# A two-layer encoder trunk: another way out of PSUM for three tiles at the end of the delta-rule layer, and the fourth weight block of the MLP split earlier

## The chip, the cores and the metric

The kernel runs on one core of a Trainium2 chip. The metric is the device time of one execution in microseconds (us). An execution here takes 1306 us; a change under 0.2% of that, 2.6 us, cannot be told from none.

## What is computed

The reference is an encoder trunk of four residual layers on an input of 512 tokens by 1024 features, in float32. Each layer is followed by a LayerNorm over a scaled residual:

```
for i in range(DEPTH):                       # DEPTH = 2
    m = _mixer_gdn(x, ...) if i % 2 == 0 else _mixer_gla(x, ...)
    x = _layernorm(DEEPNORM_ALPHA * x + m, ln1_g[i], ln1_b[i])
    x = _layernorm(DEEPNORM_ALPHA * x + _sq_relu_mlp(x, mlp_w1[i], mlp_w2[i]), ln2_g[i], ln2_b[i])

def _layernorm(x, g, b):
    mu = jnp.mean(x, axis=-1, keepdims=True)
    xc = x - mu
    var = jnp.mean(xc * xc, axis=-1, keepdims=True)
    return xc * lax.rsqrt(var + LN_EPS) * g + b

def _mixer_gdn(h, w_in, conv_w, a_log, dt_bias, norm_g, w_out):
    ...                                      # projections, convolution, chunked delta rule, per-head norm and gate
    return jnp.matmul(o.reshape(bn, s, A_VW), w_out)

def _sq_relu_mlp(h, w1, w2):
    a = jax.nn.relu(jnp.matmul(h, w1))       # w1: 1024 x 4096
    return jnp.matmul(a * a, w2)             # w2: 4096 x 1024
```

The change lies at the seam between the first mixer (the gated delta rule, "gdn") and the first MLP.

## The kernel before

**Tiles and precision.** The 512 tokens are four tiles of 128 (t = 0 to 3 here), each in two halves of 512 features. Every matrix product is done as three products of rounded halves (`mm3`): each operand is split into a high half (`xth`, `wh`, `ah`: ScalarE's cast, L102) and a low half (`xtl`, `wl`, `al`: VectorE's subtraction, L107), and TensorE adds high x high, high x low and low x high. A weight block of 512 KB is loaded by SyncE into a ring `wst` of three (`w2r` for W2), then split. The engines appear in the profile as PE (TensorE), DVE (VectorE), ACT (ScalarE), POOL (GpSimd) and SP (SyncE). Each works through its own queue in order.

**End of the delta-rule layer** (`out_last`). `z` holds alpha * x plus the part of the output projection already added. For each tile and half a PSUM bank `ob` first gets z by a product with the identity (L332), then the products of the last two heads. The bank then holds the whole sum, and `layernorm` works from it: VectorE's BN_STATS (L239) and aggregation (L240), `rsqrt` (L202 and L203 on ScalarE, L204 to L211 on VectorE), the first fold out of PSUM into `xt` (L242) and the second in place (L247). The halves come in the order t0h0, t0h1, t1h0, t1h1, t2h0, t3h0, t2h1, t3h1. `xpose` then transposes each half tile with four TensorE products (L190) into the one bank `tp`, from which ScalarE takes the high half (L193) and VectorE the low half (L194), which free the bank.

**The first MLP.** W1 comes in column blocks f0, f1, ... of 128. Three are split ahead, within the delta-rule layer (`take_ahead`); f3 is split into the MLP's own tile `ah`. The first blocks are multiplied in two halves of 256 columns, as the tiles come (tiles 0 and 1, then 2 and 3; instructions `pj`, 128x256); from f4 on a block is one product of 512 columns. ScalarE takes each from PSUM with relu into `h` (L383) and squares it (L384). VectorE forms sums of the input (`whole`, L433 to L442, in `w2r`), which are split into `xh` and `xl`; with W1 blocks p0, p1, ... and sums of blocks (L464) these give the products `fx` and `fyz`, of which the one that starts on `fx<-xh` at 460.98 us is called the sixth in this text. W2 blocks go through `w2h` and `w2l` into `pX`, `pY`, `pZ`; POOL adds some W2 blocks to others with accumulating DMAs (`w2r<-w2r`, L415). POOL also makes the masks of the next mixer in tiles of the MLP's pool (L792 to L805).

**Memory.** The delta-rule layer's tiles lie in a pool `gdn` that is closed at the end of `gdn()`; the MLP opens a pool `mlp` on the freed space. The order within an engine is made by the framework's scheduler, except where `issue_after` names an instruction behind which a piece is to be placed.

In the GLA layer `out_last` runs with `in_ps=False`: no identity product, VectorE adds z while it takes the sum out of PSUM (L338), and the variance comes from ScalarE's squares (`half_stats` L255 and L256, `norm_halves` L265 to L276).

Of the kernel before, what the change touches and what calls it, by code (L numbers as in the profile page):

```python
# [8 lines left out]
F32 = mybir.dt.float32  # L9
F32R = mybir.dt.float32r  # L10
BF16 = mybir.dt.bfloat16
F16 = mybir.dt.float16
AF = mybir.ActivationFunctionType
# [4 lines left out]
P = 128  # L18
# [10 lines left out]
class Ctx:  # L29
# [225 lines left out]
        nc.scalar.mul(v[:, 0:1], s, -1.0 / (16 * D))  # L255
        return nc.scalar.activation(junk, z, AF.Square, scale=1.0 / 32, bias=v[:, 0:1], accum_out=v[:, 1:2])  # L256

    def norm_halves(self, z, par, s, vs, order, by_dma=None):

        nc = self.nc  # L260
        V, A = nc.vector, nc.scalar
        mv = self.small.tile([P, 2], F32, name="bmv", tag="bmv")
        tv = self.small.tile([P, 2], F32, name="lnt", tag="lnt")
        rstd = self.small.tile([P, 1], F32, name="rstd", tag="rstd")
        V.scalar_tensor_tensor(mv[:, 0:1], s[:, 0:1], s[:, 1:2], self.bias[-1.0 / D], ALU.add, ALU.mult)  # L265
        A.mul(tv[:, 0:1], s[:, 1:2], -1.0 / D)
        A.activation(tv[:, 1:2], s[:, 0:1], AF.Square, scale=1.0 / D, bias=tv[:, 0:1])
        for q in order:
            V.scalar_tensor_tensor(z[q], z[q], mv[:, 0:1], par[q], ALU.add, ALU.mult)
        V.scalar_tensor_tensor(mv[:, 1:2], vs[0][:, 1:2], vs[1][:, 1:2], tv[:, 1:2], ALU.add, ALU.add)  # L270
        self.rsqrt(rstd, mv[:, 1:2], 1, LN_EPS)
        for q in range(2):
            if by_dma:
                A.mul(z[q], z[q], rstd[:, 0:1])
            else:
                self.normed = self.exped, V.scalar_tensor_tensor(z[q], z[q], rstd[:, 0:1], par[2 + q], ALU.mult, ALU.add)  # L276
        if by_dma:
            nc.gpsimd.dma_start(*by_dma, accum_op=ALU.add)
# [33 lines left out]
                    if i % piece == piece - 1:  # L312
                        yield 0.68 * piece, 0.0

    def out_last(self, w, ks, lhs, z, tags, par, homes=None, xtags=("tp",), ahead=None, in_ps=True):

        nc = self.nc
        homes = iter(homes or ())  # L320
        ws = [{k: self.wrows(w, k * P, hf * 512, next(homes, None)) for k in ks[hf][::2]} for hf in range(2)]
        if ahead:
            ahead()
        if not in_ps:
            sums = [self.small.tile([P, 2], F32, name="lns", tag="lns") for t in range(NT)]
            stats = [[self.small.tile([P, 2], F32, name=f"lnv{q}", tag=f"lnv{q}") for q in range(2)] for t in range(NT)]
        pss = {}
        for t, hf in [(t, hf) for t in range(NT - 2) for hf in range(2)] + [(NT - 2, 0), (NT - 1, 0), (NT - 2, 1), (NT - 1, 1)]:
            sl = slice(t * P, (t + 1) * P)
            ps = pss[t, hf] = self.bank([P, 512], F32, name="ob", tag=tags[hf % len(tags)])  # L330
            if in_ps:
                nc.tensor.matmul(ps, self.ident, z[t][hf], start=True, stop=False)  # L332
            for i, k in enumerate(ks[hf]):
                ah, al = lhs(k, sl)
                wh, wl = ws[hf][k - i % 2]
                self.mm3(ps, ah, al, wh[:, i % 2, :], wl[:, i % 2, :], not in_ps and i == 0, i == len(ks[hf]) - 1)
            if not in_ps:
                nc.vector.scalar_tensor_tensor(z[t][hf], ps, 1.0, z[t][hf], ALU.mult, ALU.add, accum_out=sums[t][:, hf:hf + 1])  # L338
                self.half_stats(z[t][hf], sums[t][:, hf:hf + 1], stats[t][hf], ps)
            if hf:  # L340
                if in_ps:
                    self.layernorm([pss[t, 0], pss[t, 1]], self.xh(t), par)
                else:
                    self.norm_halves(z[t], par, sums[t], stats[t], (0, 1))
                if t < NT - 2:
                    self.xpose(t, self.xt[t], xtags)
        with self.tc.issue_after(self.normed[1].ins):
            self.xpose(NT - 2, self.xt[NT - 2], xtags)
        self.xpose(NT - 1, self.xt[NT - 1], xtags)
# [478 lines left out]
def gla(c, gc, w_in, gate_w2, w_out, ln_g, ln_b, w_next):  # L828

    tc, nc = c.tc, c.nc
    H = B_H
    with c.banks(ac=2, tp=2, pj=4), tc.tile_pool(name="gla", bufs=2) as pool:
        oth = pool.tile([P, KT, S], F32R, name="oth", tag="oth", bufs=1)
        otl = pool.tile([P, KT, S], F32R, name="otl", tag="otl", bufs=1)

        gst = c.wst.tile([P, KT, 32], F32, name="gst", tag="wst")
        w_in, w_vr, w_g = w_in
        c.dma(gst, w_g)  # L840
        specs = [(c.side_by_side(gst, 32), "gps", "ac")]
        specs += [(c.wcols(w_in, c0, late=late, by_dma=True, at=64), nm, "pj")
                  for i, (c0, nm, late) in enumerate(((0, "pjq", c.late), (H * P, "pjk", c.normed)))]
        R = slice(0, 32), slice(32, 64), slice(64, 96)
        w2f = c.wst.tile([96, 2, S], F32, name="w2f", tag="wst")
        for d in range(2):
            src = gate_w2[d]
            c.dma(w2f[:, d, :], bass.AP(src.tensor, src.offset, [[0, 6]] + [list(q) for q in src.ap]))
        w2r = [pool.tile([96, S], F32R, name=f"w2r{d}", bufs=1) for d in range(2)]
        with c.in_order(mybir.EngineType.PE):  # L850
            gps, *qk0 = c.proj_halves(specs, at={(0, 2, 4 * j): lambda t=2 + j: c.xpose(t, c.xt[t], ("tp", "pj")) for j in range(2)})
        glr = []
        for d in range(2):
            nc.scalar.copy(w2r[d][0:64, :], w2f[0:64, d, :])
            nc.scalar.mul(w2r[d][R[2], :], w2f[R[2], d, :], -1.0)
            nc.gpsimd.dma_start(w2r[d][R[2], :], w2f[R[2], d, :], accum_op=ALU.add)
        for d in range(2):
            g = pool.tile([96, S], F32R, name=f"glr{d}", bufs=1)
            nc.scalar.copy(g[R[0], :], gps[R[d], :])
            nc.scalar.copy(g[R[2], :], gps[R[d], :])  # L860
            nc.vector.tensor_tensor(g[R[1], :], gps[R[d], :], g[R[0], :].bitcast(F32), ALU.subtract)
            glr.append(g)

        par = c.load_ln(ln_g, ln_b, lambda i: pool.tile([P, 512], F32, name=f"ln{i}", bufs=1))
        g = (glr, w2r, gc.gb, gc.ngb, gc.gcol)
        heads = [GlaHead(c, pool, h, (w_in, w_vr), g, gc.masks, oth, otl) for h in range(H)]
        z = [c.xh(t) for t in range(NT)]
        lhs = lambda k, sl: (oth[:, k, sl], otl[:, k, sl])
        early = list(range(KT // 2))
        with c.in_order(mybir.EngineType.PE):  # L870
            list(heads[0].qk(qk0))
            done = [heads[0].gates(d) for d in range(2)]
            def stream():
                for h in range(H):
                    yield from heads[h].vr({} if h else dict(zip((2, 3), done)))
                    yield from heads[h + 1].qk() if h + 1 < H else c.out_pieces(w_out, early, lhs, z, "pj", at=128)

            work = stream()

            def behind(n):  # L880
                for _ in range(n):
                    next(work, None)

            behind(8)
            after = None
            level = heads[0].levels()
            next(level)
            for h in range(H):
                for s in level:
                    behind((0 if h else 1) if s == 2 else 4 if s == 4 else 3)  # L890
                    if s == 8 and after:
                        after()
                    if s in (16, 32) and h + 1 < H:
                        heads[h + 1].gates(s // 32)
                level = heads[h + 1].levels() if h + 1 < H else iter(())
                heads[h].states(behind, level)
                after = heads[h].norm
            behind(2)
            after()
            behind(99)  # L900
        c.new_x()
        c.out_last(w_out, [list(range(KT // 2, KT))] * 2, lhs, z, ("pj",), par,
                   [(pool, "oah", "oal", 1), (pool, "v", "sr", 2), (pool, "F", "F", 2), (pool, "v", "sr", 2)],
                   ahead=lambda: c.take_ahead(w_next, 3), in_ps=False)


class GlaHead:
# [451 lines left out]
def gdn(c, w_in, conv_w, a_log, dt_bias, norm_g, w_out, ln_g, ln_b, x, xt, w_next):  # L1359
    tc, nc = c.tc, c.nc  # L1360
    w_in, w_g = w_in
    with c.banks(ch=2, pj=3, tp=1, ac=2), tc.tile_pool(name="gdn", bufs=1) as pool, \
# [28 lines left out]
        for i in range(A_H + 2):  # L1391
# [10 lines left out]
            if old:  # L1402
# [2 lines left out]
        c.new_x()  # L1405
        c.new_xt()
        nc.gpsimd.memset(pool.tile([P, 32], F32, name="gap", bufs=1), 0.0)
        c.out_last(w_out, [[6, 7]] * 2, lhs, z, ("pj", "ac"), par,
                   [(pool, "oah", "oal", 1), (pool, "ol", "ol", NT)], ahead=lambda: c.take_ahead(w_next, 3))


class GdnHead:
# [502 lines left out]
```

## Time and profile before

| what | value |
|---|---|
| runs | 1305.6, 1307.94, 1305.95 us; median 1305.95 |
| profiled execution, own time | 1308.32 us |
| its span, instructions | 1306.6 us, 22231 |
| PE, PE weight loads | 99%, 85% busy |
| DVE, ACT, POOL | 85%, 62%, 10% busy |
| DMA | 165.92 MB, mean 127 GB/s |

Times in the profile are us from the span's start. A row of the timeline gives start, duration, engine, line, operation, output tile <- input tiles, shape and count; what follows in brackets is the engine's idle time before it and what ended that. The delta-rule layer ends, and the MLP begins, between 386 and 470 us.

### The profile page before, as it was taken

The page shows a single profiled execution, that of the slowest core. Times are in us where ns is not written, and L with a number is a line of the kernel's source. Part 1 is how long each engine was busy: PE and PEld are TensorE (multiplying, and loading weights), DVE is VectorE, ACT ScalarE, POOL GpSimd, SP SyncE. Part 2 cuts the span into 40 slices and gives each one's busy share as a digit, 9 for nine tenths or more (in the row PEclk, how much of TensorE's full clock was granted, in tenths as well). Part 3 has the DMA queues.
Part 4 walks back from the last instruction along what each step waited for, and adds up shares of the span by engine and source line. Part 5 has one row for each costly group of instructions (what it writes and reads, how often), then busy time and mean ns, then how long its engine had stood idle before and what let it go on. Part 6 is the DMA issues. An engine that isn't in the chain of part 4 may idle for free.

```text
span 1306.6 us, 22231 instructions
## 1 busy us (share of the span) xinstructions
PE 1287.5 (99%) x8586; PEld 1105.8 (85%) x8586; DVE 1106.0 (85%) x1795; ACT 803.8 (62%) x1604; POOL 134.6 (10%) x191
## 2 busy tenths in 40 slices
PE   8999999999999999999999999999999999999996
PEld 7778888788878899999998888888889899999985
DVE  7888888988868998989989797877888789999987
ACT  4766776677543666566658754554456566666656
POOL 4000000000002810101102100000001001101021
PEclk9999999999999999999999999999999999999999
DMA  5233313233332565576647521211316376556565
GB/s 184 97 114 98 92 56 114 81 114 89 123 104 91 169 156 191 115 208 161 168 148 157 145 97 51 80 56 57 105 58 225 82 210 166 142 177 139 172 142 144
DMA packets 47805, 165.92 MB, mean 127 GB/s; under 512 B 5923, under 2 KB 6611, under 8 KB 47699
## 3 DMA queue, kind: packets, MB, share of 16 engines
q1 hardware_dynamic: 33603, 114.52, 25.5%
q0 software_dynamic: 13984, 49.95, 18.9%
q8 instruction: 67, 1.10, 0.3%
q14 instruction: 39, 0.32, 0.1%
q10 hardware_dynamic: 112, 0.03, 0.0%
HBM read 125.00 MB, written 2.65 MB: 98 GB/s over the span
## 4 chain that ended last, share of the span: by engine, by line
PE 92%; DVE 3%; ACT 2%; DMA 1%; issue 1%; SPq 0%; DVEq 0%; ACTq 0%
PE pjv L128 3%; PE pjv L129 3%; PE pX L130 3%; PE pX L129 3%; PE pjv L130 3%; PE fx L130 3%; PE pX L128 3%; PE fx L128 3%; PE fx L129 3%; PE m L1777 3%; PE fyz L130 3%; PE fyz L128 3%; PE fyz L129 3%; PE pY L129 2%; PE pY L130 2%; PE pY L128 2%
## 5 line engine op out<-in xcount | busy, mean ns | idle before, releaser
L102 ACT CAST wh<-wst 128x1024 fp32r<-128x1024 f32 x151 | 158.5, 1050 | 105.7 <-PE fyz L129 27.7
L107 DVE TENSOR_TENSOR wl<-wst,wh 128x1024 fp32r<-128x1024 f32 x149 | 183.5, 1234 | 42.1 <-ACT wh L102 42.0
L107 DVE TENSOR_TENSOR w2l<-w2r,w2h 128x1024 fp32r<-128x1024 f32 x92 | 111.6, 1225 | 20.1 <-ACT w2h L102 20.1
L102 ACT CAST w2h<-w2r 128x1024 fp32r<-128x1024 f32 x94 | 98.4, 1048 | 41.3 <-DMA w2r<-w2r 21.2
L415 POOL DMA_DIRECT2D w2r<-w2r x56 | 47.9, 887 | 491.3 <-DVE w2l L107 386.5
L464 DVE TENSOR_TENSOR wst<-wst 128x512 f32<-128x512 f32 x120 | 80.3, 691 | 0.8
L102 ACT CAST ah<-h 128x1024 fp32r<-128x1024 f32 x56 | 58.8, 1051 | 30.4 <-PE pY L129 11.6
L107 DVE TENSOR_TENSOR al<-h,ah 128x1024 fp32r<-128x1024 f32 x56 | 68.6, 1224 | 6.5 <-ACT ah L102 6.5
L130 PE MATMUL pX<-w2h,al 128*128 128x512 f32 x168 | 66.4, 395 | 0.0
L129 PE MATMUL pX<-w2l,ah 128*128 128x512 f32 x168 | 66.1, 394 | 0.0
L128 PE MATMUL pX<-w2h,ah 128*128 128x512 f32 x168 | 65.4, 389 | 0.0
L128 PE MATMUL pjv<-wh,xth 128*128 128x512 f32 x128 | 54.4, 425 | 0.0
L130 PE MATMUL fyz<-xh,wl 128*128 128x256 f32 x192 | 53.4, 278 | 0.0
L128 PE MATMUL fyz<-xh,wh 128*128 128x256 f32 x192 | 53.3, 277 | 0.0
L130 PE MATMUL fx<-xth,wl 128*128 128x256 f32 x192 | 53.2, 277 | 0.0
L129 PE MATMUL fx<-xtl,wh 128*128 128x256 f32 x192 | 53.0, 276 | 0.0
L129 PE MATMUL fyz<-xl,wh 128*128 128x256 f32 x192 | 53.0, 276 | 0.0
L130 PE MATMUL fx<-xh,wl 128*128 128x256 f32 x192 | 53.0, 276 | 0.0
L129 PE MATMUL fx<-xl,wh 128*128 128x256 f32 x192 | 53.0, 276 | 0.0
L128 PE MATMUL fx<-xth,wh 128*128 128x256 f32 x192 | 53.0, 276 | 0.0
L128 PE MATMUL fx<-xh,wh 128*128 128x256 f32 x192 | 53.0, 276 | 0.0
L129 PE MATMUL pj<-xtl,wh 128*128 128x256 f32 (+1 forms) x160 | 51.9, 325 | 0.2 <-DVE xtl L194 0.2
(543 smaller groups left out, 4320.0 us busy)
## 6 DMA issues: line engine op xcount, KB each, us to landing
wst<-in_w SPq DMA_DIRECT2D x68, 512.0 KB, 4.8
w2r<-in_w SPq DMA_DIRECT2D x60, 512.0 KB, 4.5
w2r<-w2r POOLq DMA_DIRECT2D x56, 512.0 KB, 5.9
wst<-in_a_in SPq DMA_DIRECT2D x31, 512.0 KB, 4.1
wst<-in_b_vr SPq DMA_DIRECT2D x16, 512.0 KB, 3.3
wst<-in_a_out SPq DMA_DIRECT2D x8, 512.0 KB, 4.8
wst<-in_b_in SPq DMA_DIRECT2D x8, 512.0 KB, 3.4
wst<-in_b_out SPq DMA_DIRECT2D x8, 512.0 KB, 3.2
```

The costliest lines, as they stand in the source:

```text
L102: h = nc.scalar.copy(hi, src)
L107: self.halves = h, nc.vector.tensor_tensor(lo, src, hi.bitcast(F32), ALU.subtract)
L128: mm(ps, ah, bh, start=start, stop=False, **kw)
L129: mm(ps, ah, bl, start=False, stop=False, **kw)
L130: self.last_mm = mm(ps, al, bh, start=False, stop=stop, **kw)
L415: nc.gpsimd.dma_start(blocks[a + (q,)], blocks[b + (q,)], accum_op=ALU.add)
L464: plus = lambda a, b: V.tensor_tensor(a, a, b, ALU.add)
L1777: T.matmul(ps[:, d, :], *ops(d), start=True, stop=True)
```

## The change

`out_last` gets a mode for each tile. "ps" is the way of before. In "copy" the identity product stays, but ScalarE copies the bank into `xt` with a sum on the way (L340), and the statistics are those of `half_stats` and `norm_halves`. In "add" there is no identity product: VectorE adds z out of PSUM with a sum (L344). The delta-rule layer uses ps, copy, copy, add for tiles 0 to 3. Its call also gets `later`: after tile 1's transposes a fourth W1 block (f3) is split into a tile `w3` of the pool `gdn` and handed to the MLP, which no longer splits it into its own `ah`. The GLA layer uses "add" for all tiles, as it did. Line numbers behind these places grow by 9 to 15: L383 becomes L392, L792 becomes L801, L1842 becomes L1857.

```
-    def norm_halves(self, z, par, s, vs, order, by_dma=None):
+    def norm_halves(self, z, par, s, vs, order, by_dma=None, src=None):
...
-            V.scalar_tensor_tensor(z[q], z[q], mv[:, 0:1], par[q], ALU.add, ALU.mult)
+            V.scalar_tensor_tensor(z[q], (src or z)[q], mv[:, 0:1], par[q], ALU.add, ALU.mult)
...
-    def out_last(self, w, ks, lhs, z, tags, par, homes=None, xtags=("tp",), ahead=None, in_ps=True):
+    def out_last(self, w, ks, lhs, z, tags, par, homes=None, xtags=("tp",), ahead=None, modes=("add",) * NT, later=None):
...
-            if in_ps:
+            mode = modes[t]
+            if mode != "add":
                 nc.tensor.matmul(ps, self.ident, z[t][hf], start=True, stop=False)
...
+            one = sums[t][:, hf:hf + 1]
+            if mode == "copy":
+                to = self.xh(t)[hf]
+                nc.scalar.activation(to, ps, AF.Identity, accum_out=one)
+                self.half_stats(to, one, stats[t][hf], ps)
+            elif mode == "add":
+                with self.tc.issue_after(self.last_lo.ins) if "copy" in modes else contextlib.nullcontext():
+                    nc.vector.scalar_tensor_tensor(z[t][hf], ps, 1.0, z[t][hf], ALU.mult, ALU.add, accum_out=one)
+                self.half_stats(z[t][hf], one, stats[t][hf], ps)
             if hf:
-                if in_ps:
+                if mode == "ps":
                     self.layernorm([pss[t, 0], pss[t, 1]], self.xh(t), par)
                 else:
-                    self.norm_halves(z[t], par, sums[t], stats[t], (0, 1))
+                    self.norm_halves(self.xh(t), par, sums[t], stats[t], (0, 1), src=z[t] if mode == "add" else None)
                 if t < NT - 2:
                     self.xpose(t, self.xt[t], xtags)
+                if t == 1 and later:
+                    with self.tc.issue_after(self.last_lo.ins):
+                        later()
...
+        w3 = pool.tile([P, 2, KT, P], F32R, name="w3", tag="sil", bufs=3)
+
+        def fourth():
+            c.ahead.append(c.wcols(w_next, 3 * P, pool=(None, w3[:, 0], w3[:, 1], None)))
+
         c.out_last(w_out, [[6, 7]] * 2, lhs, z, ("pj", "ac"), par,
-                   [(pool, "oah", "oal", 1), (pool, "ol", "ol", NT)], ahead=lambda: c.take_ahead(w_next, 3))
+                   [(pool, "oah", "oal", 1), (pool, "ol", "ol", NT)], ahead=lambda: c.take_ahead(w_next, 3),
+                   modes=("ps", "copy", "copy", "add"), later=fourth)
```

Where it moves instructions, first ACT's queue at the end of the delta-rule layer. `fo` and `oh` are the last heads' gated output, L202 and L203 the two parts of rsqrt, L193 the casts of the transposes. Before, up to the cast of tile 0's second half:

```order
L203 ACTIVATE rsy<-rsy 128x4
L1831 ACTIVATE fo<-op,ors 128x128 x4
L1842 CAST oh_343<-p 128x256 x2
L202 ACTIVATE rsy<-bmv,bias_75 128x1
L203 ACTIVATE rsy<-rsy 128x1
L202 ACTIVATE rsy<-bmv,bias_75 128x1
L203 ACTIVATE rsy<-rsy 128x1
L193 CAST xth<-tp 128x4x128 x3
```

And now, from `oh` to the cast of tile 0's first half (the cast of f3's high half, `w_5406<-wst`, has also come in, between L203 and `fo`):

```order
L1857 CAST oh_343<-p 128x256 x2
L340 ACTIVATE xt_5401,lns<-ob 128x512
L202 ACTIVATE rsy<-bmv,bias_75 128x1
L255 ACTIVATE lnv_5443<-lns 128x1
L340 ACTIVATE xt_5401,lns<-ob 128x512
L203 ACTIVATE rsy<-rsy 128x1
L256 ACTIVATE ob,lnv_5443<-xt_5401,lnv_5443 128x512
L255 ACTIVATE lnv_5444<-lns 128x1
L266 ACTIVATE lnt<-lns 128x1
L340 ACTIVATE xt_5402,lns<-ob 128x512
L256 ACTIVATE ob,lnv_5444<-xt_5401,lnv_5444 128x512
```

Three more small ones and the square of tile 2's first half follow before the first cast `xth`: the copies and squares of tiles 1 and 2 stand ahead of the first cast of a transpose.

Next, ACT at the start of the MLP, with the semaphores that a row waits for (DMAHW and DMASW are DMA queues of the hardware and of POOL). Before, from the first tile of the MLP's pool, `ah`, to the first `h`:

```order
L102 CAST ah<-wst 128x1024 [waits DMAHW1_49,DMASW5_49,DMAHW5_49,DMASW4_49,DMAHW6_49,DMASW3_49,DMAHW7_49,DMASW2_49,DVE_49]
L193 CAST xth<-tp 128x4x128 [waits PE_49] x3
L102 CAST w2h<-w2r 128x1024 [waits DMAHW0_49]
L102 CAST w2h<-w2r 128x1024 [waits DMAHW1_49]
L102 CAST wh<-wst 128x1024 [waits DMAHW6_49,PE_49]
L383 ACTIVATE h<-pj 128x512 [waits PE_49]
L384 ACTIVATE h<-h 128x512 [waits Activation_49]
```

And now:

```order
L193 CAST xth<-tp 128x4x128 [waits PE_49] x3
L102 CAST wh<-wst 128x1024 [waits DMAHW6_49,PE_49]
L102 CAST wh<-wst 128x1024 [waits DMAHW7_49,PE_49]
L102 CAST wh<-wst 128x1024 [waits DMAHW0_49,PE_49]
L392 ACTIVATE h<-pj 128x512 [waits DMASW4_49,DMASW3_49,DMASW5_49,DMASW2_49,DMAHW1_49,DVE_49,PE_49]
L392 ACTIVATE h<-pj 128x512
L393 ACTIVATE h<-h 128x512 [waits Activation_49] x2
L392 ACTIVATE h<-pj 128x512 x2
L393 ACTIVATE h<-h 128x512 [waits Activation_49] x2
L102 CAST ah<-h 128x1024 [waits Activation_49]
L102 CAST w2h<-w2r 128x1024 [waits DMAHW4_49]
```

The casts of f4, f5 and f6 now stand ahead of the first four `h`, and the long list of waits, which is that of the first use of the MLP's pool, has moved from `ah` to the first `h`. In it PE's count is the one of the last product that reads `w3` (f3, tiles 2 and 3). The same count stands on DVE's first row of the MLP (L387, before L378), on POOL's first mask (L801) and on SP's first `w2r`.

On SP, four more W1 loads have moved ahead of the first W2 loads.

DVE's queue from tile 2's last folds to the low halves of its transposes (L194) and the MLP's first sums. Before (`al` is f3's low half):

```order
L247 SCALAR_TENSOR_TENSOR xt_5402<-xt_5402,rstd,lnp 128x512 x2
L205 SCALAR_TENSOR_TENSOR rst<-bmv,rst 128x1
L206 TENSOR_SCALAR rst<-rst 128x1
L211 TENSOR_TENSOR rstd<-rsy,rst 128x1
L247 SCALAR_TENSOR_TENSOR xt_5403<-xt_5403,rstd,lnp 128x512 x2
L194 TENSOR_TENSOR xtl<-tp,xth 128x4x128
L378 MEMSET gap 128x8
L378 MEMSET gap 128x24
L107 TENSOR_TENSOR al<-wst,ah 128x1024
L194 TENSOR_TENSOR xtl<-tp,xth 128x4x128 x3
L433 TENSOR_TENSOR w2r<-xth,xtl 128x1024 x3
```

And now (`w_5406` is f3's low half; `qd` and `z` hold tile 3's residual):

```order
L194 TENSOR_TENSOR xtl<-tp,xth 128x4x128
L107 TENSOR_TENSOR w_5406<-wst,w_5406 128x1024
L344 SCALAR_TENSOR_TENSOR qd,lns<-ob,qd 128x512
L276 SCALAR_TENSOR_TENSOR xt_5402<-xt_5402,rstd,lnp 128x512
L344 SCALAR_TENSOR_TENSOR z,lns<-ob,z 128x512
L265 SCALAR_TENSOR_TENSOR bmv<-lns,bias_83 128x1
L269 SCALAR_TENSOR_TENSOR xt_5403<-qd,bmv,lnp 128x512
L269 SCALAR_TENSOR_TENSOR xt_5403<-z,bmv,lnp 128x512
L270 SCALAR_TENSOR_TENSOR bmv<-lnv_5447,lnv_5448,lnt 128x1
```

Four small rows of rsqrt follow, then:

```order
L276 SCALAR_TENSOR_TENSOR xt_5403<-xt_5403,rstd,lnp 128x512 x2
L194 TENSOR_TENSOR xtl<-tp,xth 128x4x128 x4
L107 TENSOR_TENSOR wl<-wst,wh 128x1024 x3
L387 MEMSET gap 128x8
L387 MEMSET gap 128x24
L442 TENSOR_TENSOR w2r<-xth,xtl 128x1024 x4
```

The four low halves of tiles 2 and 3 (L194) stood behind tile 3's last fold before too. What has come in ahead of them, behind the low half of tile 1's second transpose (the first row), is f3's low half, the two adds and both folds of tile 3; and the splits of f4 to f6 now stand ahead of the MLP's first rows (L387, L442). From about a quarter of the first MLP on, the queues of all engines have the order of before again.

More of the change, by code (lines that the diff above doesn't have):

```diff
@@ L323, in out_last @@
             ahead()
-        if not in_ps:
-            sums = [self.small.tile([P, 2], F32, name="lns", tag="lns") for t in range(NT)]
-            stats = [[self.small.tile([P, 2], F32, name=f"lnv{q}", tag=f"lnv{q}") for q in range(2)] for t in range(NT)]
+        sums = [self.small.tile([P, 2], F32, name="lns", tag="lns") for t in range(NT)]
+        stats = [[self.small.tile([P, 2], F32, name=f"lnv{q}", tag=f"lnv{q}") for q in range(2)] for t in range(NT)]
         pss = {}
@@ L335, in out_last @@
                 wh, wl = ws[hf][k - i % 2]
[L336 to L339, printed above, removed]
+                self.mm3(ps, ah, al, wh[:, i % 2, :], wl[:, i % 2, :], mode == "add" and i == 0, i == len(ks[hf]) - 1)
+            one = sums[t][:, hf:hf + 1]
[7 more added lines that the diff above has]
+                self.half_stats(z[t][hf], one, stats[t][hf], ps)
             if hf:
-                if in_ps:
+                if mode == "ps":
                     self.layernorm([pss[t, 0], pss[t, 1]], self.xh(t), par)
                 else:
-                    self.norm_halves(z[t], par, sums[t], stats[t], (0, 1))
+                    self.norm_halves(self.xh(t), par, sums[t], stats[t], (0, 1), src=z[t] if mode == "add" else None)
                 if t < NT - 2:
                     self.xpose(t, self.xt[t], xtags)
+                if t == 1 and later:
+                    with self.tc.issue_after(self.last_lo.ins):
+                        later()
         with self.tc.issue_after(self.normed[1].ins):
@@ L903, in gla @@
                    [(pool, "oah", "oal", 1), (pool, "v", "sr", 2), (pool, "F", "F", 2), (pool, "v", "sr", 2)],
-                   ahead=lambda: c.take_ahead(w_next, 3), in_ps=False)
+                   ahead=lambda: c.take_ahead(w_next, 3))
 class GlaHead:
```

## The prediction

> **What bounds the kernel now.** I read the busy table and the chain of work first, then the windows of the stretch that the change touches, then that stretch instruction by instruction.
>
> ```profile
> PE 1287.5 (99%) x8586; PEld 1105.8 (85%) x8586; DVE 1106.0 (85%) x1795; ACT 803.8 (62%) x1604; POOL 134.6 (10%) x191
> PE 92%; DVE 3%; ACT 2%; DMA 1%; issue 1%; SPq 0%; DVEq 0%; ACTq 0%
> ```
>
> PE is busy 99% of the span and is 92% of the chain. So time falls only by the PE work removed, and every wait that PE gains is added whole: almost no idle time later can take it up.
>
> The windows (length, then busy us and count for PE, PEld, DVE, ACT, POOL):
>
> ```profile
> 390.00:400.00 10.00, 9.87 (x38) 6.32 (x37) 8.03 (x21) 2.93 (x10) 0.00 (x0) 1.00 0.25 94
> 400.00:410.00 10.00, 10.00 (x59) 7.73 (x59) 9.73 (x24) 2.85 (x6) 0.00 (x0) 1.00 0.01 2
> 410.00:420.00 10.00, 10.00 (x86) 9.67 (x84) 7.89 (x19) 3.31 (x6) 4.94 (x8) 1.00 0.39 147
> 430.00:440.00 10.00, 10.00 (x55) 8.69 (x54) 10.00 (x9) 8.48 (x12) 9.35 (x10) 1.00 0.36 112
> ```
>
> From 390 to 420 the delta-rule layer ends: DVE is nearly full at 400 to 410, ACT at 30%. From 430 to 440, in the MLP, DVE has no gap at all. PE waits for nobody in either.
>
> The third thing to read is how the MLP's memory pool opens (start, duration, engine, instruction; in brackets the idle time before it and its releaser; the last row is SP's total wait, times and longest):
>
> ```profile
> 413.45 1.42 DVE L247 SCALAR_TENSOR_TENSOR xt<-xt,rstd,lnp 128x512 f32<-128x512 f32 x2
> 414.89 1.05 ACT L102 CAST ah<-wst 128x1024 fp32r<-128x1024 f32 x1 [1.20 <-DVE xt L247]
> 415.06 0.35 POOL L792 MEMSET tmp<- 128x128 f32 x2 [43.50 <-DVE xt L247]
> SPq L52 <- DVE xt L247: 24.6, 1, 24.6
> 424.81 0.59 ACT L383 ACTIVATE h<-pj 128x512 f32<-128x512 f32 x1
> ```
>
> The first tile of the MLP pool that each engine touches waits for the same instruction, the last LayerNorm half (ends 414.87), the last reader of the delta-rule layer's pool. The new pool opens for everyone at once.
>
> **The change, part by part.**
>
> *Identity products.* Tile 3 loses its two.
>
> ```profile
> 398.73 1.02 PE L332 MATMUL ob<-qd,ident 128*128 128x512 f32 x2
> L332 PE MATMUL ob<-z,ident x8: 590/591/592, 388.1 to 404.6; 128*128 128x512 f32 x8
> 400.29 0.60 PE L190 MATMUL tp<-ident,xt 128*128 128x128 f32 x4
> ```
>
> Each is two passes. From 398.73 the identity product and three products of 0.23 fill the 1.56 us to the transposes at 400.29, so it costs 0.87. Two of them: **-1.73 us**, on PE and so on the path.
>
> *New statistics.* ACT gets four copies out of PSUM, which before does not show, and six squares with small operations; DVE gets two adds (L344) for eight BN_STATS less six, and the fold operations. Prices from the GLA layer, where the same helper runs:
>
> ```profile
> 961.53 0.69 ACT L256 ACTIVATE ob<-xt,lnv 128x512 f32<-128x512 f32 x1
> 962.16 0.19 ACT L256 ACTIVATION_READ_ACCUMULATOR ob<-xt,lnv 128x1 f32 x1
> 962.25 0.18 ACT L255 ACTIVATE lnv<-lns 128x1 f32<-128x1 f32 x1
> 960.56 0.69 DVE L338 SCALAR_TENSOR_TENSOR xt<-ob,xt 128x512 f32<-128x512 f32 x1 [0.74 <-PE ob L130]
> ```
>
> A square with its sum takes ACT 0.72 from start to start (961.53 to 962.25). A copy out of PSUM with a sum lies between the 0.59 of the h row above, which has no sum, and 0.72; I take 0.72, because it has the accumulator's read. So ACT gains about 4 x 0.72 + 6 x 0.72 + 12 small ones at 0.15, 9 us in a stretch where it was idle for 20. That is cheap in amount, not in place: the in-order queue now holds six of these and seven small ones ahead of the first transpose's cast (xth L193), 5.7 us (6 x 0.72 + 7 x 0.2) that start only when tile 1's first bank is done. DVE's sum moves by 6 x 0.7 less (statistics) and 2 x 0.69 + 1.2 more (adds, and the low half of the fourth weight block, which came at 415.98 before): -1.6 us of some 28. It gets hardly emptier.
>
> *Walking the transposes.* All four tiles' transposes share one PSUM bank: the next may start only when both casts of the last are done. First cast from about 402.1 (copy of tile 1 at 396.4, plus 5.7), with the cast's 0.59 and the low half's 0.69 the second transpose starts at 403.4, where before has 402.29. The third and fourth come at 406.2 and 408.7 (before 405.10 and 407.19), each behind two L269 or L276 (0.7 each) that now stand ahead of the low half on DVE. Tile 2's second transpose waits for a low half that stands behind tile 3's whole chain on DVE. That was so before (the L247 row above, to 414.87), but the chain now starts later and holds more (low half of the weight 1.2, two adds 1.5, two L269 1.5, four small 0.8, two L276 1.4, the low half 0.7, and waits for the squares): from 411 to about 419.5. Before:
>
> ```profile
> 402.29 0.66 PE L190 MATMUL tp<-ident,xt 128*128 128x128 f32 x4
> 420.09 0.66 PE L190 MATMUL tp<-ident,xt 128*128 128x128 f32 x4
> 432.30 0.40 PE L128 MATMUL pj<-xth,wh 128*128 128x512 f32 x1
> ```
>
> The last transpose then starts near 423.5, and what follows it (92 products of 256 columns at 0.118, the pace from 420.94 to 432.30 in 96) ends at 434 to 435, I take 434.5. Before this point was 432.30. So this part is **+2.2 us**, the -1.73 within it: about 3.9 us of new waits on PE. Bounds: with no wait at all 430.6, at my slowest reading of each step 435.1.
>
> *The pool.* The fourth weight block now lives in the delta-rule layer's pool and is read by PE until exactly this point. By the handover seen above, ACT's first h, DVE's sums, SP's first w2r loads and POOL's masks all move from 415 to 425 to 434.5. Ahead of it stand only the loads of W1 and the splits of its blocks f4 to f6.
> First, the next column block needs a free bank, and that is given by the first h: 0.59 plus both ends, **+0.9 us** on PE.
> Second, DVE. From 422 on it was full in before and reached the sixth product's low half only just in time:
>
> ```profile
> 434.62 1.31 DVE L107 TENSOR_TENSOR w2l<-w2r,w2h 128x1024 fp32r<-128x1024 f32 x1
> 442.36 3.77 DVE L107 TENSOR_TENSOR xl<-w2r,xh 128x1024 fp32r<-128x1024 f32 x3
> 450.27 1.05 ACT L102 CAST w2h<-w2r 128x1024 fp32r<-128x1024 f32 x1 [4.88 <-DMA w2r<-in_w]
> 460.05 1.22 DVE L107 TENSOR_TENSOR wl<-wst,wh 128x1024 fp32r<-128x1024 f32 x1
> 461.21 0.28 PE L130 MATMUL fx<-xh,wl 128*128 128x256 f32 x1
> ```
>
> PE's product at 461.21 uses the low half that ends at 461.27. In the new order DVE's way from the release to that low half is: four sums (4.9), a wait to +6.8 for the first w2h (ACT does eight h and squares, ah and the cast first), seven operations (9.1), one sum and four xl at 1.23 (6.2), the low half and the pair's sums (4.8 to 26.9), then a w2l that needs a W2 block loaded only when the third xl frees its buffer (the 450.27 row waited for that load too), al, h and the low half: 30.1 to 31.3 after the release. PE wants it at 0.9 + (461.21 - 432.30) = 29.8. **+1.1 us** (0.3 to 1.5).
> The operations in that sum are 1.23 to 1.40 from start to start, as while POOL worked, against 1.14 after it. The Trainium skill, "SBUF — State Buffer", section "Who interferes with whom", says that a DVE instruction with two SBUF inputs contends with a GpSimd instruction that reads SBUF; the rows agree (1.31 and 1.48 against 1.22). POOL now works over the same 34 us as this chain, so the slow pace stands; at the fast one the third term would be nothing and the sum 3.1.
>
> *POOL's own chain.* Its masks took 34.2 us, then come the accumulating DMAs:
>
> ```profile
> 449.26 1.84 POOL L415 DMA_DIRECT2D w2r<-w2r  x2
> 454.40 0.84 POOL L415 DMA_DIRECT2D w2r<-w2r  x1 [3.29 <-DMA w2r<-w2r]
> 466.02 1.04 ACT L102 CAST w2h<-w2r 128x1024 fp32r<-128x1024 f32 x1
> 478.41 1.05 ACT L102 CAST w2h<-w2r 128x1024 fp32r<-128x1024 f32 x1 [1.74 <-DMA w2r<-w2r]
> ```
>
> The first landed by 454.40, 5.1 us after issue. Now: 434.5 + 34.2 + 5.1 = 473.8. The cast that reads it, at 466.02 before, would come at 470.2: ACT stops for 3.6 us, with a cast of a W1 half behind it that PE needs at 476.4 and gets, through DVE, at 475.5 to 476.7. The second pair of loads then meets the last accumulations. Between 0 and 1.5; **+0.3 us**.
>
> Sum: 2.2 + 0.9 + 1.1 + 0.3 = **+4.5 us**. The profiled execution's own time is 1308.32 (span 1306.6), 2.4 above the median of 1305.95; the difference is carried over to the median: **1310.5**. No change cannot be told from 0.2%, 2.6 us.
>
> **Rivals.**
> *Relief.* DVE is the engine that is full where the tiles leave PSUM, and ACT takes its statistics: tiles come out no later than before and no PE wait is new. The release is then at 430.6, the next block waits 0.9 (431.5, -0.8), and product six is 0.3 to 1.5 late: 1305.4 to 1306.7. If W1's fourth block does not hold the pool (every first touch then comes before PE asks), only -1.73 is left: 1304.2, the side of faster, though just within what can be told. For it: ACT's 30% in the windows. Against: the casts of the transposes sit in the same ACT queue. The Trainium skill, "Perfetto Trace Analysis", section "Optimizing Scalar/DVE Operations", says that offloading to Scalar may make sense when DVE is saturated; by it this rival would be the likely one, and 97% of DVE at 400 to 410 is its condition.
> *Cascade.* POOL's DMAs land late enough to hold ACT's casts each time: the landing of the third pair passes what PE has as cover (4.5 us at 478.41) and each of three rounds adds 1.5: 1314 to 1316. It decides from a first landing later than 475.
> *Late chain only.* The waits at the transposes as forecast, but the bank and product six hidden (DVE at its fast pace): 1308.2.
>
> **How the numbers follow.** Sum as worked (1308.6 to 1313): 0.52. Relief with the pool held: 0.18; relief without: 0.08. Cascade: 0.13. Late chain only: 0.09. Faster by over 0.2% (below 1303.3) is the upper part of the relief without, 0.05, since PE has no more than 1.73 to give and the runs of before scatter by 2.3; slower (above 1308.6) is the sum and the cascade, 0.65; the rest, 0.30, is the same. The range leaves out half of the cascade and the lowest relief: 1304.8 to 1314.3.
>
> **What would show it.** In the new trace: first h, first mask and first w2r load all right behind the last product with the fourth block, at about 434.5; a PE wait of 0.9 ahead of f4; PE waits of 0.5 to 1 ahead of transposes, released by the low-half casts; a wait at product six for wl. I am wrong if the first h comes before 425, if PE has no waits before 432, or if PE waits mainly for DMA w2r after 470.

## The result, and the profile after

The change costs 8.4 us. Median of six runs: 1314.49 us (1313.31 to 1315.08), against 1306.11 for six runs of the kernel before; ratio 1.0064, interval 1.0054 to 1.0074. The direction was forecast, the size was not: +4.5 was expected.

The busy line of the profiled execution (span 1313.3 us, TensorE's mean granted clock 0.997 against 0.996) and its chain of work:

```profile
PE 1286.2 (98%) x8582; PEld 1103.7 (84%) x8582; DVE 1105.6 (84%) x1796; ACT 811.0 (62%) x1636; POOL 135.0 (10%) x191
PE 86%; DVE 5%; ACT 3%; POOL 3%; DMA 2%; issue 1%; SPq 0%; DVEq 0%; POOLq 0%; ACTq 0%
```

PE does 1.3 us less work, and its share of the chain falls from 92% to 86%. POOL, which was not in the chain, now has 3% of it. To see where PE lost the time I mark the same six products in every kernel (the first identity product; f4's first product; an `fyz` right behind the sixth product; two later `fyz`; an `fx` at 549) and compare the stretches between them. Windows of the kernel after, then of before, cut at those marks (length, then busy us and count of PE, PEld, DVE, ACT, POOL):

```profile
385.09:432.53 47.44, 44.36 (x290) 37.13 (x288) 32.99 (x74) 23.64 (x68) 0.58 (x3) 1.00 0.22 69
432.53:464.27 31.74, 30.47 (x151) 25.68 (x151) 31.19 (x28) 22.86 (x32) 30.19 (x33) 1.00 0.49 166
464.27:478.15 13.88, 13.88 (x92) 12.42 (x90) 11.78 (x17) 7.67 (x12) 5.29 (x8) 1.00 0.85 193
478.15:507.46 29.31, 26.04 (x164) 22.50 (x164) 26.24 (x32) 16.98 (x24) 3.37 (x4) 1.00 0.81 203
507.46:555.60 48.14, 48.14 (x314) 43.48 (x313) 44.58 (x57) 30.12 (x43) 3.43 (x4) 1.00 0.53 148
```

```profile
386.53:432.30 45.77, 45.64 (x293) 38.04 (x292) 39.97 (x78) 20.20 (x43) 16.75 (x20) 1.00 0.31 106
432.30:462.34 30.04, 30.04 (x152) 25.49 (x151) 27.86 (x27) 18.97 (x25) 19.22 (x23) 1.00 0.74 202
462.34:476.10 13.76, 13.76 (x93) 12.46 (x92) 13.03 (x19) 9.05 (x13) 1.68 (x2) 1.00 0.23 65
476.10:500.85 24.75, 24.75 (x165) 22.42 (x163) 22.02 (x29) 15.75 (x23) 1.69 (x2) 1.00 0.87 228
500.85:549.00 48.15, 48.15 (x315) 43.48 (x314) 44.28 (x56) 30.12 (x43) 3.44 (x4) 1.00 0.52 142
```

The stretches grow by +1.67, +1.70, +0.12, +4.56 and -0.01 us: 8.0 in all, and nothing after. (The two spans differ by 6.7 only, because the profiled execution of before reached the first mark 1.4 us later; its granted clock was 0.50 from 10.0 to 13.4 us.) PE had 0.13 us idle in the whole of this part before; now it has 3.08, 1.27 and 3.27 in three of the stretches. These sums are what I compare below. In the kernels that follow they stand 0.2 to 1.3 us under the difference of the medians, once 1.9, so a difference under 1 us in them decides nothing here.

The waits of PE from 380 to 520 (who waits, for whom; total, times, longest). The same view of before lists none:

```profile
PE tp L190 <- DVE xtl L194: 1.5, 3, 0.9
PE fx L128 <- ACT h L515: 1.5, 1, 1.5
PE fx L130 <- DVE wl L107: 1.3, 1, 1.3
PE pX L128 <- DVE xt L546: 1.0, 1, 1.0
PE pj L128 <- ACT xth L193: 0.9, 2, 0.7
PE pj L128 <- ACT h L392: 0.7, 1, 0.7
PE fyz L128 <- ACT h L532: 0.6, 1, 0.6
```

The pool opens as forecast; timeline rows of ACT, POOL, SP's queue and PE:

```profile
431.88 1.09 ACT L392 ACTIVATE h<-pj 128x512 f32<-128x512 f32 x2 [1.82 <-PE pj L130]
431.95 0.35 POOL L801 MEMSET tmp<- 128x128 f32 x2 [61.85 <-PE pj L130]
431.96 2.06 SPq L52 DMA_DIRECT2D w2r<-in_w  x4
432.53 0.50 PE L128 MATMUL pj<-xth,wh 128*128 128x512 f32 x1 [0.69 <-ACT h L392]
```

First `h`, first mask and first W2 load start within 0.1 us, all behind the last product that reads `w3`. And the 4.56 us, in the timeline of POOL, ACT, DVE and PE:

```profile
466.52 1.84 POOL L424 DMA_DIRECT2D w2r<-w2r  x2 [0.27 <-DMA wst<-in_w]
473.17 1.05 ACT L102 CAST w2h<-w2r 128x1024 fp32r<-128x1024 f32 x1 [4.69 <-DMA w2r<-w2r]
484.69 1.05 ACT L102 CAST w2h<-w2r 128x1024 fp32r<-128x1024 f32 x1 [5.66 <-DMA w2r<-w2r]
485.77 1.23 DVE L107 TENSOR_TENSOR w2l<-w2r,w2h 128x1024 fp32r<-128x1024 f32 x1 [3.04 <-ACT w2h L102]
489.17 0.37 ACT L515 COPY h<-fx 128x256 f32<-128x256 f32 x1
489.59 0.39 PE L128 MATMUL fx<-xh,wh 128*128 128x256 f32 x1 [1.50 <-ACT h L515]
```

POOL's first accumulating DMAs, issued at 449.26 before, are issued at 466.52, behind 34 us of masks. ACT's cast of what they add stands in its in-order queue and holds it for 4.69 us, and a later one for 5.66. Behind the later cast stand the casts for DVE (idle 3.04) and the copies that empty the `fx` and `fyz` banks; so PE, which has nothing to do with that DMA, waits for a bank.

### The profile page after: what moved, and what is told of

Read it like the earlier page. It is cut to its first block, busy times and chain, and to the rows that moved or that the text cites. A ratio compares the mean times of both kernels' runs of the same rounds, so it can differ in the third digit from the quotient of the medians.

```text
span 1313.3 us, 22251 instructions
## 1 busy us (share of the span) xinstructions
PE 1286.2 (98%) x8582; PEld 1103.7 (84%) x8582; DVE 1105.6 (84%) x1796; ACT 811.0 (62%) x1636; POOL 135.0 (10%) x191
## 4 chain that ended last, share of the span: by engine, by line
PE 86%; DVE 5%; ACT 3%; POOL 3%; DMA 2%; issue 1%; SPq 0%; DVEq 0%; POOLq 0%; ACTq 0%
PE pjv L128 3%; PE pjv L129 3%; PE pjv L130 3%; PE pX L130 3%; PE pX L129 3%; PE pX L128 3%; PE fx L130 3%; PE fx L128 3%; PE fx L129 3%; PE m L1792 3%; PE fyz L130 2%; PE fyz L128 2%; PE fyz L129 2%; PE scp L1017 2%; PE pY L129 2%; PE pY L130 2%
## 5 line engine op out<-in xcount | busy, mean ns | idle before, releaser
L128 PE MATMUL pj<-xth,wh 128*128 128x256 f32 (+1 forms) x160 | 51.2, 325 | 1.6 <-ACT xth L193 0.9
```

The source lines that it names most:

```text
L128: mm(ps, ah, bh, start=start, stop=False, **kw)
```

## Experiments: the parts alone

**The three modes without the fourth block** (edit of the call):

```
-                   modes=("ps", "copy", "copy", "add"), later=fourth)
+                   modes=("ps", "copy", "copy", "add"))
```

> The new ways out of PSUM alone; the fourth W1 block is split in the MLP's own tile, as before. Pool theory (the fourth block, in the delta-rule layer's pool, keeps the MLP's pool shut until 432 us, and this costs 6 to 7 of the 8.4 us): the pool opens near 417, POOL's masks end near 451, the accumulating DMAs come as before; left are 1.7 us saved and about 2.4 us of waits at the transposes: 1305.5 to 1308. Rival, ACT theory (the copies and squares in ACT's queue make all casts late, the pool is incidental): 1311 to 1314.5.

Measured: 1307.67, ratio 1.0013 (1.0005 to 1.0022); at the marks +1.13, all of it ahead of f4. POOL's first mask in the timeline, and PE's largest waits from 380 to 520:

```profile
414.45 0.35 POOL L801 MEMSET tmp<- 128x128 f32 x2 [44.95 <-DVE xt L276]
```

```profile
PE tp L190 <- DVE xtl L194: 0.7, 1, 0.7
PE tp L190 <- DVE gap L387: 0.5, 1, 0.5
PE pj L130 <- DVE al L107: 0.4, 1, 0.4
```

The pool opens at 414 again, and everything behind f4 is as before. The modes alone cost 1 to 2 us, though two identity products are gone.

**The fourth block without the modes:** `modes=("ps",) * NT, later=fourth`.

> The fourth block alone, early and in the delta-rule layer's pool; all four tiles leave PSUM as before. Pool theory: the first h, the first mask and the first w2r load wait for the last product of the fourth block, near 432; waits of 0.7 us ahead of f4, 1 to 2 at the sixth product, and 3 to 5 for accumulating DMAs after 480: 1311 to 1314.5. ACT theory: no change, 1305 to 1307.5.

Measured: 1314.17, ratio 1.0064 (1.0050 to 1.0078); at the marks +2.14 to f4, +1.70 to the sixth product, +3.97 behind 476, in all +7.81. First `h`, first mask and the cast that holds ACT:

```profile
432.31 1.09 ACT L392 ACTIVATE h<-pj 128x512 f32<-128x512 f32 x2 [1.94 <-PE pj L130]
432.39 0.35 POOL L801 MEMSET tmp<- 128x128 f32 x2 [62.30 <-PE pj L130]
484.56 1.05 ACT L102 CAST w2h<-w2r 128x1024 fp32r<-128x1024 f32 x1 [5.52 <-DMA w2r<-w2r]
```

Nearly the whole loss comes with the fourth weight block alone, and no tile need leave PSUM in another way for it. The parts don't add up (1.1 + 7.8 against 8.0).

**The fourth block, read earlier.** In the second halves of the first four products (tiles 2 and 3) f3 comes first instead of last, so that `w3` is let go sooner; all else is the kernel after.

```
-            for i, (ps, ((wh, wl), _, _)) in enumerate(zip(out, specs)):
+            turn = list(enumerate(zip(out, specs)))
+            if hf and len(self.ahead) == 4 and len(specs) == 4:
+                turn = turn[3:] + turn[:3]
+            for i, (ps, ((wh, wl), _, _)) in turn:
```

> The changed kernel with one thing turned: in the second half of the first four products (tiles 2 and 3) the fourth block comes first instead of last. Nothing is removed; only the last reader of the delta-rule layer's pool comes three products (3 x 24 x 0.118 = 8.5 us) earlier, near 424. Pool theory: first h, masks, w2r loads move to 424, the masks end near 458, the first accumulations land near 463, before the cast that wants them; the waits ahead of f4, at the sixth product and after 476 go: 1306 to 1308.5. Rival (two more casts and a subtraction for the fourth block in a full stretch, or the order of the casts that the scheduler made for it): 1312 to 1314.5.

Measured: 1309.08 against 1306.41, ratio 1.0020 (1.0011 to 1.0028). At the marks +1.18 to f4, +0.66 to the sixth product, 0.00 behind it. First `h` and first accumulating DMAs in the timeline, then ACT's waits for them from 464 to 512:

```profile
423.53 0.60 ACT L395 ACTIVATE h<-pj 128x512 f32<-128x512 f32 x1 [2.40 <-PE pj L130]
457.46 1.83 POOL L427 DMA_DIRECT2D w2r<-w2r  x2
```

```profile
ACT w2h L102 <- DMA w2r<-w2r: 4.4, 2, 2.3
```

The same row of the kernel after, and of before:

```profile
ACT w2h L102 <- DMA w2r<-w2r: 10.6, 3, 5.7
```

```profile
ACT w2h L102 <- DMA w2r<-w2r: 3.8, 2, 2.1
```

The release comes 39.1 us after the first identity product (423.53 less 384.39) instead of 46.8. With the same memory, the same DMAs and the same masks, these 7.7 us give back 5.7 of the 8.4 us lost, a little less than the 1308.5 forecast at most. So when `w3` is read for the last time decides the later loss.

The edit moved more than the release, though. From about 460 us on, the queues of ACT and DVE have the order of the kernel before again, while the kernel after, the fourth block alone and the two kernels with moved masks below share another one, which the scheduler made for them. What the earlier release gives and what the old order gives is not separated by this run.

## Experiments: POOL's masks out of the way

If the DMAs are late because they stand behind the masks, moving the masks behind the first eight DMAs must take that away:

```
+            if gi == 0 and extra:
+                with tc.issue_after(adds[7].ins):
+                    extra(lambda: pool.tile([P, P], F32, name="tmp", tag="tmp", bufs=2))
```

> The changed kernel, with POOL's masks put behind the first eight accumulating DMAs, so that these no longer wait 34 us behind the masks. If the masks in front of the DMAs are what costs the 4.4 us after 480: these go, and the wait of 1.3 at the sixth product too if DVE's operations are faster without POOL beside them: 1308 to 1310.5. If the DMAs are late for another reason (their own loads, the order of the casts on ACT): 1313 to 1315.

Measured: 1312.68, ratio 1.0052 (1.0039 to 1.0064). The wait at the sixth product is gone (+0.16 there, +1.70 in the kernel after) and the DMAs are early (the first at 441.72), with ACT's longest wait for them 2.0. Yet 2.97 us are lost behind 476, and the time lies between the two forecasts. Timeline rows of DVE beside the masks, which now lie at 485.5 to 516, and just ahead of them, then PE's wait:

```profile
483.74 1.22 DVE L107 TENSOR_TENSOR al<-h,ah 128x1024 fp32r<-128x1024 f32 x1
486.83 1.62 DVE L591 SCALAR_TENSOR_TENSOR h<-h 128x1024 f32<-128x1024 f32 x1
489.78 1.62 DVE L107 TENSOR_TENSOR wl<-wst,wh 128x1024 fp32r<-128x1024 f32 x1
502.69 0.50 PE L128 MATMUL pX<-w2h,ah 128*128 128x512 f32 x1 [1.53 <-DVE xt L547]
```

So the masks cost in two ways: they hold POOL's DMAs, and they slow DVE. An instruction of this size with two inputs in SBUF takes up to 1.62 beside them and 1.22 without. The Trainium skill, "SBUF — State Buffer", section "Who interferes with whom", calls the port pair that the two engines share an exclusive lock; the rows bear out that they contend, as a stretching by up to a third here.

**The same edit in the kernel before**, as a control.

> Control: the kernel before with the same move of the masks. There PE had no wait between 386 and 660 us, so nothing can be gained: 1305 to 1307.5 by both theories. More than 2.6 us off would mean that the move does something of its own.

Measured: 1307.0, ratio 1.0007 (0.9998 to 1.0015), at the marks +0.03. Where the pool opened early, the masks had slack at either place.

**Masks behind the sixteenth DMA** (`gi == 1`, `adds[15]`).

> The changed kernel with the masks put into POOL's free stretch 80 us further on (behind the sixteenth accumulating DMA). With the masks right behind the eighth, 3.0 us were left after 485, where DVE's operations took 1.5 to 1.6 us instead of 1.22 beside the masks. If that was the masks' doing, nothing is left after f4 but 1.8 us: 1307.5 to 1309.5. If DVE's or ACT's order is what costs there: 1311.5 to 1313.5.

Measured: 1310.85, between the two forecasts; ratio 1.0033 (1.0021 to 1.0044). At the marks +2.68 to f4, +0.18 to the sixth product, +1.34 behind 476. About 1.0 of the first is a clock dip (below). Of PE's waits behind 432, this one is left, and beside it a row of DVE:

```profile
PE pX L128 <- DVE xt L547: 1.0, 1, 1.0
```

```profile
486.35 1.22 DVE L591 SCALAR_TENSOR_TENSOR h<-h 128x1024 f32<-128x1024 f32 x1
```

No mask runs there, and DVE's rows are at 1.22. DVE's queue order shows why this `xt` is late: from the low half `w2l` at 485.20 to this fold at 499.76 DVE has no gap and works 14.56 us; before, the same way (483.89 to 496.26) took 12.37. It now holds two sums of `h` (L591 and L593, 1.14 us each from start to start) that before ran earlier, at 481.77 and 462.92. They account for the difference; that the kernel loses its last 1.3 us by this order is read from the traces, and no run tests it alone. With the masks away, the loss behind f4 falls from 6.4 to 1.5 us, so masks and DMAs together are three quarters of it.

A variant with `w3` in a pool of its own was not tried.

## Experiments: the end of the delta-rule layer

Why do the modes lose 1 us, when they remove 1.73 us of PE work? First the "add" alone, `modes=("ps", "ps", "ps", "add")`, without the fourth block.

> Tile 3 alone by VectorE without identity products, tiles 0 to 2 as before, the fourth block in the MLP. ACT has no copies and only two squares. If the copies cost the waits at the transposes (2.9 us with copies): the 1.7 us are gained, 1303.5 to 1305. If DVE's chain for tile 3 costs them: 1305.5 to 1307.5.

Measured: 1307.14, ratio 1.0009 (1.0001 to 1.0018), at the marks +0.18. PE's waits from 380 to 425:

```profile
PE pj L128 <- ACT xth L193: 0.7, 1, 0.7
PE tp L190 <- DVE xt L247: 0.3, 1, 0.3
PE tp L190 <- DVE xtl L194: 0.2, 1, 0.2
```

To f4, PE is busy 1.1 us less than before (44.51 against 45.64) and idle 1.3 us more, 1.2 of it listed: what was saved came back as waits. (Here the two adds may run ahead of tile 1's transposes; in the change they are placed behind them.) Then the copies alone, `("ps", "copy", "copy", "ps")`.

> Tiles 1 and 2 by ScalarE's copies, tiles 0 and 3 as before, the fourth block in the MLP. All identity products are there, so nothing can be gained on PE. If the copies cost the waits at the transposes: 1307.5 to 1309.5. If not: 1305 to 1306.5.

Measured: 1307.27, between the two forecasts; ratio 1.0005 (0.9996 to 1.0014), at the marks +0.42. So tile 2's and tile 1's statistics on ACT relieve nobody who is waited for. The Trainium skill, "Perfetto Trace Analysis", section "Optimizing Scalar/DVE Operations", says that offloading to Scalar may make sense when DVE is saturated. DVE was (9.73 of 10 us at 400 to 410 before), but here it brought nothing measurable; as I read it, because the rows that free the transposes' bank still stand in DVE's queue.

The far end, all four tiles with "add" and no identity product at all, `modes=("add",) * NT`:

> All four tiles by VectorE without identity products, the fourth block in the MLP. PE has 6.9 us less (8 x 0.87). If the identity products were work on the path: 1300 to 1302. If the stretch goes at the pace of DVE's chain and the identity products only filled PE's time beside it (tile 3 alone gave 1.7 and got 0.2 worse): 1304.5 to 1308.

Measured: 1311.01 against 1306.45, above both forecasts; ratio 1.0033 (1.0021 to 1.0045). Its window from 395 to 405 (columns as above) and PE's largest wait from 380 to 425:

```profile
395.00:405.00 10.00, 7.23 (x35) 5.38 (x33) 9.88 (x34) 8.15 (x32) 0.00 (x0) 1.00 0.00 1
```

```profile
PE tp L190 <- DVE xt L276: 3.6, 2, 2.3
```

PE idles 2.8 of 10 us while DVE is full. This stretch goes at the pace of DVE's LayerNorm, and the identity products had only filled PE's time while it waited: from its first product to f4 PE idles 7.35 us, 7.2 more than before, which takes up the 6.9 us of removed work. Most of the loss on top is the clock's. After idle time the granted clock is 0.50 at 391.4 to 394.8 and at 405.0 to 411.8, for example here:

```profile
409.00:411.00 2.00, 2.00 (x9) 1.99 (x10) 2.00 (x7) 0.79 (x4) 0.00 (x0) 0.50 0.00 0
```

PE is busy for 7.0 us at that clock, so about half of it, 3.5 us, is lost (an estimate from these figures), of 3.9 us by which the way to f4 grew.

My rival for the waits was the single bank `tp` of the transposes. Three kernels give them three banks under two tags, `xtags=("tp", "ch")`: with "add" for tile 3, with the modes of the change, and with "add" for all; none has the fourth block.

> Tile 3 alone by VectorE, and the transposes go in turn to two tags of PSUM, tp and the free banks ch, three banks in place of one. If the waits at the transposes (1.2 us listed with tile 3 alone) come from the one bank: they go and the 1.7 us show, 1304 to 1305.5. If PE waits for the LayerNorm itself: 1305.5 to 1307.

> The modes of the change (ps, copy, copy, add), the fourth block in the MLP, transposes in three banks. One bank theory: 1304 to 1306, against 1307.7 with one bank. LayerNorm theory: 1306.5 to 1308.5.

> All four tiles by VectorE, transposes in three banks. If one bank is what turned the removed identity products into waits: 1300 to 1303. If DVE's chain sets the pace: as with one bank, within 1.5 us.

Measured: 1311.88, ratio 1.0040 (1.0028 to 1.0053); 1311.9, 1.0039 (1.0027 to 1.0052); 1312.58, 1.0045 (1.0033 to 1.0058). The first two lie above both forecasts and are slower than their fellows with one bank (1.0009 and 1.0013); the third is not faster than its own (1.0033). PE's longest wait in each, in that order:

```profile
PE pj L128 <- DVE rst L204: 2.2, 1, 2.2
```

```profile
PE pj L128 <- ACT ob L256: 3.4, 1, 3.4
```

```profile
PE tp L190 <- DVE xt L276: 5.1, 2, 3.8
```

Part of these times is again the clock: it is 0.50 for 3.4, 3.4 and 10.2 us, which costs about 1.7, 1.7 and 3.7 us of PE's work (estimated as above). But PE's idle time up to f4 rose too, to 3.9, 4.4 and 8.3 us, from 1.4, 2.3 and 7.4 with one bank. So the theory of the one bank fell. In the first two PE now waits ahead of the MLP's first `pj`; that this `pj` lacks a bank which the transposes took is my reading, which no run tests. In the third the wait is for the LayerNorm itself. No kernel here beats the one before.

## Why the prediction was wrong in size

- **POOL's own chain, +0.3: the step that failed.** The stretch behind 478 measured +4.56. I had the right picture (masks of 34.2 us, then DMAs with ACT's casts behind them) and let the cover of PE absorb it. The sum gave a stop of ACT of 3.6 and a first landing 87.3 us after the first identity product (473.8 less 386.53); measured are 4.69 and 88.1 (473.17 less 385.09). For this first round the cover held: 464 to 478 grew by only 0.12. What I named but did not price is the second round. Before, rounds lay apart: two DMAs issued at 449.26 (landed 5.1 us later), the next pair at 473.78. Now 466.52 and 478.34 with singles between: the first landed 6.65 us after issue, the second pair 6.35, and ACT stopped for 5.66, with PE's waits of 1.5 and 0.6 for ACT behind it. The DMA engines were fully busy while the second pair was on its way, 76% before; that this made it slower is my reading. About 1.3 of the 4.56 are not POOL's: they stayed when the masks were far away, and go with the order of DVE's queue. The rival Cascade came nearest. Its size (1314 to 1316, measured 1314.49) is partly luck, since it had three rounds of 1.5 each; its deciding point, a landing later than 475 (88.5 after the first identity product), was set 0.4 too late. The prediction named PE waiting for these DMAs after 470 as a sign that it would be wrong; PE does, by way of ACT's queue.
- **Identity products and transposes, +2.2, with the bank +0.9: 3.1 forecast, 1.67 measured.** The waits are where I said (the transposes behind `xtl`, f4 behind `h`), but 3.1 us are listed where I summed 3.9 + 0.9. The first cast started 14.7 us after the first identity product, where I had 15.6; this earliness runs through, and the release came 46.8 after it instead of 48.0.
- **Sixth product, +1.1 (0.3 to 1.5): 1.70 measured**, just above its bounds. The reason held: with the masks moved and DVE's queue in the same order, the wait was gone (+0.16) and DVE's rows of that size took 1.22 instead of up to 1.48, so POOL beside DVE is what makes this product late.
- **The pool's handover** was right to the row: `h`, masks and W2 loads open together behind f3's last product.
- **Relief, with or without the pool held, did not happen.** DVE's busy time to f4 fell (39.97 to 32.99, of which a part is work moved behind f4), but PE's idle time rose from 0.13 to 3.08. Late chain only would need the rest hidden, which it was not.

In short: two terms too large by 1.4, one too small by 0.6, and one too small by 4.3; together 3.5 of the 4.0 us between the forecast and the median.

## What to carry to other kernels

A tile that is put into an old pool for convenience also sets when the next pool opens, for all engines at once: read the last reader of every tile that you add there, and if you must add one, let it be read first. When a wait is moved later, follow the in-order queue behind the waiting instruction through the second and third round, since rounds that were apart before may now meet. And work taken off a full engine is worth something only if the rows that the bottleneck waits for move with it.

## What was unexpected in the hardware

TensorE's granted clock fell after one of two pauses that looked alike. Both kernels have PE half idle from 402 to 406 (busy 2.09 and 2.08 of 4 us). First the kernel with masks behind the sixteenth DMA, then the kernel after (the figure behind POOL's is the clock):

```profile
402.71:406.12 3.41, 1.51 (x9) 1.07 (x10) 3.34 (x10) 1.59 (x7) 0.00 (x0) 1.00 0.01 2
406.00:408.00 2.00, 2.00 (x12) 2.00 (x11) 1.82 (x5) 0.59 (x1) 0.00 (x0) 0.53 0.04 12
```

```profile
401.64:405.05 3.41, 1.92 (x11) 1.13 (x9) 3.37 (x8) 2.81 (x10) 0.00 (x0) 1.00 0.01 2
406.00:408.00 2.00, 2.00 (x17) 1.93 (x17) 1.87 (x6) 0.59 (x1) 0.00 (x0) 1.00 0.05 12
```

Only the first loses its clock: 0.50 for 3.41 us, and about 1 us of time at the marks. The Trainium skill, "TensorE: Matmul & The Clock Gate", section "What's actually happening", says that the clock falls after an idle window of about 3.4 us, and that the window is free-running. The traces agree on the window: all falls of one execution lie whole multiples of 3.413 us apart (in the first kernel 406.12 and 1300.41, 262 of them). But the window need not be idle: PE was busy for 1.51 us of the one ahead of the fall. The second kernel's windows, counted back from its fall at 1306.17, lie otherwise, and the one with the pause has 1.92 us busy. Of the windows at full clock in the 14 traces, every one with at most 1.51 us busy is followed by a half clock, none with more than 2.10 is, and in between it goes either way. So a wait of some 2 us near the bottleneck can cost another 1 us, or nothing, depending on how it falls into these windows.
